# Pre-norm weights as columns on the transposed x, and x / rms made by ScalarE, in a two-layer decoder trunk

## The chip, the core and the metric

The kernel runs on one core of a Trainium2 chip. The metric is the device time of one execution, in microseconds: lower is better. The engines work side by side, each through its own queue in order: TensorE (PE, with its weight loads as PEld) multiplies matrices into PSUM, VectorE (DVE) and ScalarE (ACT) work elementwise, GpSimd (POOL) makes the inverse roots, and SyncE (SP) only issues DMAs.

## The reference

One sequence of 512 tokens with 1024 channels in float32 goes through two layers of three residual stages. The first and third are SwiGLU feed-forward blocks with 2816 hidden channels, the second a mixer of attention, a short convolution and a pooling branch. Each stage is wrapped in two RMS norms, one ahead of it and one behind it, each with weights g per channel:

```python
def _rmsnorm(x, g):
    x32 = x.astype(jnp.float32)
    y = x32 * lax.rsqrt(jnp.mean(x32 * x32, axis=-1, keepdims=True) + RMS_EPS)
    return (y * g.astype(jnp.float32)).astype(x.dtype)
...
    for l in range(DEPTH):
        g = norm_g[l]
        f = _swiglu(_rmsnorm(x, g[0]), ffn_w_gate[l, 0], ffn_w_up[l, 0], ffn_w_down[l, 0])
        x = x + 0.5 * _rmsnorm(f, g[1])
        m = _mixer(_rmsnorm(x, g[2]), w_in[l], conv_w[l], pool_w[l], pool_scale[l], w_out[l])
        x = x + _rmsnorm(m, g[3])
        f = _swiglu(_rmsnorm(x, g[4]), ffn_w_gate[l, 1], ffn_w_up[l, 1], ffn_w_down[l, 1])
        x = x + 0.5 * _rmsnorm(f, g[5])
```

## The kernel before

The residual x stays in SBUF as four token tiles of 128 tokens by 1024 channels. A stage needs the normed x with channels on the partitions, so each token tile is transposed by TensorE. Every float32 matrix is split into a high part (rounded to TensorE's float32r format) and the rest, and a product is three matmuls: high by high, high by rest, rest by high (`mm3`). For the normed x the parts are `hHs` (named hh in the trace) and `hLs` (hl); for weights wh and wl.

**Weights and slots.** All weights come in 324 units of up to 128 x 1024. `load` (L145 to L149) issues a unit's DMA on SP into a slot named raw, `split` makes wh with ScalarE (L156) and wl with VectorE (L157). There are 28 slots of 512 KB for raw, wh, wl, the parts of hidden activations, accumulators f, and the norm weights. A ledger in Python counts them while the program is written: `ahead` loads a unit while more slots are free than `slots["reserve"]`, and splits one while at least two more are free than that; it runs whenever slots are given back (`give`). This fixes the order in which loads and splits stand in the program. The order of the instructions in each queue is then settled when the program is built; for TensorE it is chained by hand (`after`), in the order of the listing.

**A stage's end.** There are six ends; the change touches the five that have a stage behind them. In the feed-forward block the last chunk, in the mixer the second half of the output projection (`OUT_B`), runs token tile by token tile (`by_tokens`), each tile in two halves of 512 channels. `Boundary` loads the post-norm weights (`self.post`) and the weights of the norm ahead of the next stage (`self.g`), each a 128 x 1024 tile with the same row in all partitions (`gain`, L207 to L211, 512 KB, one slot). For each half tile `store` adds the last product to f (L363), sums squares with ScalarE (L364) and multiplies by the post weights (L367). `finish` makes the mean (L373), the inverse root on POOL (`root`, L314) and adds to x (L377), and calls `prenorm`: two squares with sums by ScalarE (L322), x times the weights (L323), the mean (L324), the root, and the scaling (L326), all into f's slot. `turned` runs as a side task 13 us of matmuls later (`D_TURN`): eight transposes (L267) in two groups of four into PSUM banks, a ScalarE copy to hh (L335) and a VectorE subtraction to hl (L336) for each group. Then it gives back f's slot, and with the last tile those of the two weight tiles.

**The stage behind** a mixer end is a feed-forward block. Its first three pairs of units run on token tiles 0 and 1 alone before they run on 2 and 3 (`HEAD`), so hh and hl of tiles 0 and 1 must exist when it starts. Behind a feed-forward stage of the same layer the mixer takes one token tile at a time.

**The first norm** (`first`, at the start) already works in another way: x / rms is transposed without weights, and a column of weights per channel group, from the tile `cst`, is multiplied on the way out of PSUM (L818), before the copy (L820) and the subtraction (L821).

Of the kernel before, what the change touches and what calls it, by code (L numbers as in the profile page):

```python
# [15 lines left out]
P = 128  # L16
# [8 lines left out]
DEPTH = 2  # L25
# [33 lines left out]
C_G0 = C_PSC + DEPTH * 2  # L59
C_END = C_G0 + KB  # L60

# [41 lines left out]
def trunk_kernel(ctx: ExitStack, tc: tile.TileContext, xt: bass.AP, wu: bass.AP,  # L103
# [81 lines left out]

    cst = cpool.tile([P, 64], F32, name="cst")[:, :C_END]
    x = cpool.tile([P, TBS, D], F32, name="x")
# [128 lines left out]

    def prenorm(key, tb, g, buf, free):

        ss, ms = small(), small()
        for dh in range(2):  # L320
            s = slice(dh * DH, (dh + 1) * DH)
            nc.scalar.activation(tmp(), x[:, tb, s], AF.Square, scale=D ** -0.5, accum_out=ss[:, dh:dh + 1])  # L322
        nc.vector.tensor_tensor(buf, x[:, tb, :], g, op=ALU.mult)  # L323
        nc.vector.scalar_tensor_tensor(ms[:, 0:1], ss[:, 0:1], EPS, ss[:, 1:2], op0=ALU.add, op1=ALU.add)  # L324
        r = root(ms[:, 0:1])
        nc.vector.tensor_scalar(buf, buf, r, None, op0=ALU.mult)  # L326

        def turned():
            for q in range(2):
                ps = bank()  # L330
                for i in range(4):
                    turn(ps[:, i * P:(i + 1) * P], buf[:, (4 * q + i) * P:(4 * q + i + 1) * P])
                pv = ps.rearrange("p (a b) -> p a b", a=4)
                dst = (slice(None), slice(4 * q, 4 * q + 4), tok(tb))
                nc.scalar.copy(hHs[dst], pv)  # L335
                nc.vector.tensor_tensor(hLs[dst], pv, f32(hHs[dst]), op=ALU.subtract)  # L336
            done((key, "h", tb))
            free()
            return
            yield  # L340

        side(turned(), D_TURN)

    class Boundary:


        def __init__(self, n, l, i, pre):
            self.key, self.pre = n + 1, pre
            self.post = gain(l, i + 1)
            self.g = gain(*pre) if pre is not None else None  # L350

            factor = 1.0 if i == 2 else 0.5
            self.scale, self.eps = D ** -0.5 / factor, EPS / factor ** 2
            self.left = TBS
            self.ss, self.fg = {}, {}
# [15 lines left out]
        def finish(self, tb, f):  # L371
# [8 lines left out]
            if self.pre is not None:  # L380
                prenorm(self.key, tb, self.g, f, self.free)

        def free(self):
            self.left -= 1
            slots["reserve"] += 1
            give(1 if self.left else 3)

# [53 lines left out]
    def ffn(n_, l, i, pre, next_reserve):  # L441
# [13 lines left out]
        for c, n in enumerate(CHUNKS):  # L455
            last = c == len(CHUNKS) - 1
            if last:
                slots["reserve"] += 2 if pre is not None else 1
                bd = Boundary(n_, l, i, pre)
# [135 lines left out]
    def mixer(key, l, i, pre):  # L595
# [179 lines left out]
        need((key, "mix"))  # L775
        slots["reserve"] += 2
        give(TBS)
# [26 lines left out]
    def first(tb, buf):  # L804
# [6 lines left out]

        for q in range(2):
            ps = bank()
            for i in range(4):
                turn(ps[:, i * P:(i + 1) * P], buf[:, (4 * q + i) * P:(4 * q + i + 1) * P])
            g = cst[:, C_G0 + 4 * q:C_G0 + 4 * q + 4].unsqueeze(2).to_broadcast((P, 4, P))
            t = tmp().rearrange("p (a b) -> p a b", a=4)
            nc.vector.tensor_tensor(t, ps.rearrange("p (a b) -> p a b", a=4), g, op=ALU.mult)  # L818
            dst = (slice(None), slice(4 * q, 4 * q + 4), tok(tb))
            nc.scalar.copy(hHs[dst], t)  # L820
            nc.vector.tensor_tensor(hLs[dst], t, f32(hHs[dst]), op=ALU.subtract)  # L821
        if tb == 0:
# [71 lines left out]
def _pack_consts(norm_g, conv_w, pool_scale):  # L894
# [8 lines left out]
    c[:, C_PSC:C_PSC + DEPTH * 2] = pool_scale.reshape(DEPTH * 2, P).T  # L903
    c[:, C_G0:C_G0 + KB] = norm_g[0, 0].reshape(KB, P).T
    return c
# [37 lines left out]
```

## Time and profile before

| | us |
|---|---|
| median of 3 runs | 1924.6 |
| lowest and highest | 1923.42, 1925.09 |
| the profiled execution, its time | 1924.39 |
| its span, first to last instruction | 1922.6 |
| VectorE, ScalarE and POOL busy | 875.8, 719.6, 44.6 |

The page of the profile gives the busy time of each engine, its share in 40 equal slices of the span and the granted clock of TensorE (1.00 is 2.4 GHz, 0.50 is 1.2 GHz). A timeline lists instructions in order of time; a bracket behind one gives the idle time of its engine just before it and what ended that. Matmuls overlap, so a row's duration is longer than the distance to the next start. Names are those of the program without buffer numbers; L12 is line 12.

### The profile page before, as it was taken

The page shows a single profiled execution, that of the slowest core. Times are in us where ns is not written, and L with a number is a line of the kernel's source. Part 1 is how long each engine was busy: PE and PEld are TensorE (multiplying, and loading weights), DVE is VectorE, ACT ScalarE, POOL GpSimd, SP SyncE. Part 2 cuts the span into 40 slices and gives each one's busy share as a digit, 9 for nine tenths or more (in the row PEclk, how much of TensorE's full clock was granted, in tenths as well). Part 3 has the DMA queues.
Part 4 walks back from the last instruction along what each step waited for, and adds up shares of the span by engine and source line. Part 5 has one row for each costly group of instructions (what it writes and reads, how often), then busy time and mean ns, then how long its engine had stood idle before and what let it go on. Part 6 is the DMA issues. An engine that isn't in the chain of part 4 may idle for free.

```text
span 1922.6 us, 22108 instructions
## 1 busy us (share of the span) xinstructions
PE 1887.2 (98%) x9078; PEld 1590.5 (83%) x9078; DVE 875.8 (46%) x1158; ACT 719.6 (37%) x1129; POOL 44.6 (2%) x68
## 2 busy tenths in 40 slices
PE   7999999999999999999999999999999999999998
PEld 6888888888878888888898888888888888888887
DVE  5323333567767323333463223337577663223333
ACT  4323222357764323222243322224477542322221
POOL 0000000000001000000000000000000010000000
PEclk8999999999999999999999999999999999999999
DMA  5223232131123223223142322423211232222311
GB/s 196 99 73 125 77 117 103 44 132 55 38 88 127 93 72 121 84 102 121 44 153 78 109 88 77 142 77 107 70 50 44 83 142 89 99 88 88 132 66 44
DMA packets 50501, 179.65 MB, mean 93 GB/s; under 512 B 5728, under 2 KB 5856, under 8 KB 50400
## 3 DMA queue, kind: packets, MB, share of 16 engines
q1 hardware_dynamic: 50400, 178.24, 26.8%
q8 instruction: 71, 1.16, 0.2%
q14 instruction: 30, 0.25, 0.0%
HBM read 176.12 MB, written 2.10 MB: 93 GB/s over the span
## 4 chain that ended last, share of the span: by engine, by line
PE 90%; DVE 6%; ACT 1%; issue 1%; DMA 1%; POOL 0%; SPq 0%; DVEq 0%; POOLq 0%; ACTq 0%
PE psz L225 78%; PE psd L225 11%; DVE wl L157 1%; DMA g<-in_gains_dram 1%; PE psd L267 1%; DVE f L363 1%; DVE x L377 1%; DVE f L323 1%; ACT t L298 0%; DMA raw<-in_w_dram 0%; DVE pL L514 0%; DVE hl L336 0%; ACT pH L513 0%; POOL ss L314 0%; ACT t L543 0%
## 5 line engine op out<-in xcount | busy, mean ns | idle before, releaser
L225 PE MATMUL psz<-hh,wh 128*128 128x512 f32 (+1 forms) x1536 | 569.0, 370 | 7.0 <-ACT hh L335 4.2
L225 PE MATMUL psz<-hl,wh 128*128 128x512 f32 (+1 forms) x1536 | 568.4, 370 | 5.4 <-DVE hl L336 4.3
L225 PE MATMUL psz<-hh,wl 128*128 128x512 f32 (+1 forms) x1536 | 567.8, 370 | 0.0
L157 DVE TENSOR_TENSOR wl<-raw,wh 128x1024 fp32r<-128x1024 f32 x324 | 386.9, 1210 | 313.9 <-ACT wh L156 245.8
L225 PE MATMUL psz<-wh,hid 128*128 128x512 f32 x1408 | 437.4, 390 | 0.0
L156 ACT CAST wh<-raw 128x1024 fp32r<-128x1024 f32 x324 | 328.8, 1039 | 224.0 <-PE psz L225 177.9
L225 PEld LDWEIGHTS psz<-hh,wh 128*128 128x128 f32 x1536 | 293.6, 191 | 55.6 <-ACT hh L335 5.1
L225 PEld LDWEIGHTS psz<-hl,wh 128*128 128x128 f32 x1536 | 293.6, 191 | 53.3 <-DVE hl L336 5.0
L225 PEld LDWEIGHTS psz<-hh,wl 128*128 128x128 f32 x1536 | 293.4, 191 | 47.1
L225 PEld LDWEIGHTS psz<-wh,hid 128*128 128x128 f32 x1408 | 264.5, 188 | 54.6
L449 DVE TENSOR_TENSOR t<-t,psz 128x512 f32<-128x512 f32 x84 | 57.7, 687 | 479.4 <-PE psz L225 479.4
L225 PE MATMUL psz<-wl,hid 128*128 128x512 f32 x704 | 274.3, 390 | 0.0
L450 ACT CAST hid<-t 128x512 fp32r<-128x512 f32 x88 | 54.6, 620 | 450.8 <-DVE t L449 450.8
L298 ACT ACTIVATE t<-psz 128x512 f32<-128x512 f32 (+1 forms) x136 | 77.4, 573 | 236.0 <-PE psz L225 235.1
L225 PEld LDWEIGHTS psz<-wl,hid 128*128 128x128 f32 x704 | 132.3, 188 | 27.0
L225 PE MATMUL psd<-hh,wh 128*128 128x512 f32 (+1 forms) x320 | 119.8, 374 | 0.0
L225 PE MATMUL psd<-hh,wl 128*128 128x512 f32 (+1 forms) x320 | 118.2, 369 | 0.0
L225 PE MATMUL psd<-hl,wh 128*128 128x512 f32 (+1 forms) x320 | 118.1, 369 | 0.0
L451 DVE TENSOR_TENSOR hid<-t,hid 128x512 fp32r<-128x512 f32 x88 | 61.0, 693 | 60.8 <-ACT hid L450 60.8
L314 POOL TENSOR_TENSOR ss<-ss,expo 128x1 f32<-128x1 f32 x48 | 36.1, 752 | 1691.9 <-DVE ss L373 1582.6
L225 PEld LDWEIGHTS psd<-hl,wh 128*128 128x128 f32 x320 | 60.5, 189 | 10.1 <-issue 0.5
L225 PEld LDWEIGHTS psd<-hh,wl 128*128 128x128 f32 x320 | 60.4, 189 | 10.2
(106 smaller groups left out, 1435.4 us busy)
## 6 DMA issues: line engine op xcount, KB each, us to landing
raw<-in_w_dram SPq DMA_DIRECT2D x316, 512.0 KB, 3.3
g<-in_gains_dram SPq DMA_DIRECT2D x11, 512.0 KB, 5.1
x<-in_xt_dram SPq DMA_DIRECT2D x4, 512.0 KB, 6.9
raw<-in_w_dram SPq DMA_DIRECT2D x8, 256.0 KB, 2.8
out_dram<-x SPq DMA_DIRECT2D x8, 256.0 KB, 2.1
mat<-in_mats_dram SPq DMA_DIRECT2D x1, 384.0 KB, 9.1
mat<-in_mats_dram SPq DMA_DIRECT2D x1, 64.0 KB, 3.2
cst<-in_consts_dram SPq DMA_DIRECT2D x1, 29.0 KB, 3.2
```

Of the source, the lines that this page charges most:

```text
L156: nc.scalar.copy(h[:, :n], raw[:, :n])
L157: nc.vector.tensor_tensor(lo[:, :n], raw[:, :n], f32(h[:, :n]), op=ALU.subtract)
L225: ins = nc.tensor.matmul(dst, w, r, start=start, stop=stop, skip_group_check=True)
L267: ins = nc.tensor.transpose(dst, src, ident)
L298: ins = nc.scalar.activation(out_, in_, f_, **kw)
L314: nc.gpsimd.tensor_tensor(r, ms, expo, op=ALU.pow)
L323: nc.vector.tensor_tensor(buf, x[:, tb, :], g, op=ALU.mult)
L363: nc.vector.tensor_tensor(f[:, s], f[:, s], ps, op=ALU.add)
L377: nc.vector.scalar_tensor_tensor(xs, self.fg.pop((tb, dh)), r, xs, op0=ALU.mult, op1=ALU.add)
L449: nc.vector.tensor_tensor(u, g, pu, op=ALU.mult)
L450: nc.scalar.copy(t[:, 0, :], u)
L451: nc.vector.tensor_tensor(t[:, 1, :], u, f32(t[:, 0, :]), op=ALU.subtract)
```

## The change

The weights of all six norms ahead of a stage now lie as columns in `cst`, which grows from 58 to 98 columns. `prenorm` no longer multiplies by the weights and makes x / rms with one ScalarE activation (identity with the root as a scale per token) instead of VectorE's L326. The way out of PSUM that `first` had becomes `turned_parts`, used by `turned` as well: VectorE multiplies each group of four transposes by its columns into a temporary tile, ScalarE copies that to hh, VectorE subtracts to hl. `Boundary` loads no pre-norm weights; the ledger reserves one slot at a stage's end instead of two, and the last token tile gives back two instead of three.

```diff
--- before.py
+++ after.py
@@ -57,7 +57,7 @@
 C_CONV = C_INV16 + 2 * PAD
 C_PSC = C_CONV + DEPTH * 2 * 3
 C_G0 = C_PSC + DEPTH * 2
-C_END = C_G0 + KB
+C_END = C_G0 + DEPTH * 3 * KB
 
 M_ID, M_TRI, M_MASK, M_POOL = 0, P, 2 * P, 3 * P
 M_END = M_POOL + DEPTH * 2 * P
@@ -183,7 +183,7 @@
 
 
 
-    cst = cpool.tile([P, 64], F32, name="cst")[:, :C_END]
+    cst = cpool.tile([P, 128], F32, name="cst")[:, :C_END]
     x = cpool.tile([P, TBS, D], F32, name="x")
     mat = cpool.tile([P, M_END], F32, name="mat")
     hHs = cpool.tile([P, KB, T], F32R, name="hh")
@@ -314,26 +314,32 @@
         nc.gpsimd.tensor_tensor(r, ms, expo, op=ALU.pow)
         return r
 
-    def prenorm(key, tb, g, buf, free):
+    def turned_parts(n, tb, buf):
+
+        for q in range(2):
+            ps = bank()
+            for i in range(4):
+                turn(ps[:, i * P:(i + 1) * P], buf[:, (4 * q + i) * P:(4 * q + i + 1) * P])
+            o = C_G0 + n * KB + 4 * q
+            g = cst[:, o:o + 4].unsqueeze(2).to_broadcast((P, 4, P))
+            t = tmp().rearrange("p (a b) -> p a b", a=4)
+            nc.vector.tensor_tensor(t, ps.rearrange("p (a b) -> p a b", a=4), g, op=ALU.mult)
+            dst = (slice(None), slice(4 * q, 4 * q + 4), tok(tb))
+            nc.scalar.copy(hHs[dst], t)
+            nc.vector.tensor_tensor(hLs[dst], t, f32(hHs[dst]), op=ALU.subtract)
+
+    def prenorm(key, tb, buf, free):
 
         ss, ms = small(), small()
         for dh in range(2):
             s = slice(dh * DH, (dh + 1) * DH)
             nc.scalar.activation(tmp(), x[:, tb, s], AF.Square, scale=D ** -0.5, accum_out=ss[:, dh:dh + 1])
-        nc.vector.tensor_tensor(buf, x[:, tb, :], g, op=ALU.mult)
         nc.vector.scalar_tensor_tensor(ms[:, 0:1], ss[:, 0:1], EPS, ss[:, 1:2], op0=ALU.add, op1=ALU.add)
         r = root(ms[:, 0:1])
-        nc.vector.tensor_scalar(buf, buf, r, None, op0=ALU.mult)
+        nc.scalar.activation(buf, x[:, tb, :], AF.Identity, scale=r)
 
         def turned():
-            for q in range(2):
-                ps = bank()
-                for i in range(4):
-                    turn(ps[:, i * P:(i + 1) * P], buf[:, (4 * q + i) * P:(4 * q + i + 1) * P])
-                pv = ps.rearrange("p (a b) -> p a b", a=4)
-                dst = (slice(None), slice(4 * q, 4 * q + 4), tok(tb))
-                nc.scalar.copy(hHs[dst], pv)
-                nc.vector.tensor_tensor(hLs[dst], pv, f32(hHs[dst]), op=ALU.subtract)
+            turned_parts(key, tb, buf)
             done((key, "h", tb))
             free()
             return
@@ -347,7 +353,6 @@
         def __init__(self, n, l, i, pre):
             self.key, self.pre = n + 1, pre
             self.post = gain(l, i + 1)
-            self.g = gain(*pre) if pre is not None else None
 
             factor = 1.0 if i == 2 else 0.5
             self.scale, self.eps = D ** -0.5 / factor, EPS / factor ** 2
@@ -378,12 +383,12 @@
                 if self.pre is None:
                     nc.sync.dma_start(out=out[:, tb, dh * DH:(dh + 1) * DH], in_=xs)
             if self.pre is not None:
-                prenorm(self.key, tb, self.g, f, self.free)
+                prenorm(self.key, tb, f, self.free)
 
         def free(self):
             self.left -= 1
             slots["reserve"] += 1
-            give(1 if self.left else 3)
+            give(1 if self.left else 2)
 
 
     def token_mms(ps, tb, src, blocks, w, dh_first, dh_last):
@@ -455,7 +460,7 @@
         for c, n in enumerate(CHUNKS):
             last = c == len(CHUNKS) - 1
             if last:
-                slots["reserve"] += 2 if pre is not None else 1
+                slots["reserve"] += 1
                 bd = Boundary(n_, l, i, pre)
             src = {}
             j = 0
@@ -773,7 +778,7 @@
         by_halves(OUT_A, mixed, store)
         give(3)
         need((key, "mix"))
-        slots["reserve"] += 2
+        slots["reserve"] += 1
         give(TBS)
         load_set(18)
         bd = Boundary(key, l, i, pre)
@@ -809,16 +814,7 @@
         r = root(ms[:, 0:1])
         nc.vector.tensor_scalar(buf, x[:, tb, :], r, None, op0=ALU.mult)
 
-        for q in range(2):
-            ps = bank()
-            for i in range(4):
-                turn(ps[:, i * P:(i + 1) * P], buf[:, (4 * q + i) * P:(4 * q + i + 1) * P])
-            g = cst[:, C_G0 + 4 * q:C_G0 + 4 * q + 4].unsqueeze(2).to_broadcast((P, 4, P))
-            t = tmp().rearrange("p (a b) -> p a b", a=4)
-            nc.vector.tensor_tensor(t, ps.rearrange("p (a b) -> p a b", a=4), g, op=ALU.mult)
-            dst = (slice(None), slice(4 * q, 4 * q + 4), tok(tb))
-            nc.scalar.copy(hHs[dst], t)
-            nc.vector.tensor_tensor(hLs[dst], t, f32(hHs[dst]), op=ALU.subtract)
+        turned_parts(0, tb, buf)
         if tb == 0:
             ps = bank("z")
             for _ in range(WARM // 4):
@@ -901,7 +897,7 @@
             c[rows, C_INV16 + b * PAD:C_INV16 + (b + 1) * PAD] = 1.0 / np.minimum(np.arange(1, PAD + 1), w)
     c[:, C_CONV:C_CONV + DEPTH * 6] = conv_w.reshape(DEPTH, 3, 2, P).transpose(3, 0, 2, 1).reshape(P, DEPTH * 6)
     c[:, C_PSC:C_PSC + DEPTH * 2] = pool_scale.reshape(DEPTH * 2, P).T
-    c[:, C_G0:C_G0 + KB] = norm_g[0, 0].reshape(KB, P).T
+    c[:, C_G0:C_END] = norm_g[:, 0::2].reshape(DEPTH * 3 * KB, P).T
     return c
```

## Rows read from the trace of the kernel before

**Rows 1.** The page, part 1: busy us, share of the span, instructions, by engine.

```profile
PE 1887.2 (98%) x9078; PEld 1590.5 (83%) x9078; DVE 875.8 (46%) x1158; ACT 719.6 (37%) x1129; POOL 44.6 (2%) x68
```

**Rows 2.** Table by stretch: us, busy us (instructions) of five engines, granted clock, DMA.

```profile
30.00:378.00 348.00, 348.00 (x1653) 294.03 (x1653) 120.83 (x135) 97.24 (x130) 2.08 (x3) 0.99 0.26 90
...
560.00:624.00 64.00, 59.84 (x330) 52.51 (x330) 44.65 (x63) 32.27 (x62) 7.13 (x8) 0.95 0.41 144
...
1505.00:1570.00 65.00, 60.62 (x336) 53.04 (x337) 45.68 (x65) 32.45 (x63) 7.14 (x8) 0.97 0.40 142
```

**Rows 3.** TensorE's timeline at both mixer ends: start us, us, instruction, idle before and releaser.

```profile
599.26 1.03 PE L267 MATMUL psd<-mat,f 128*128 128x128 f32 x8
...
600.59 0.40 PE L225 MATMUL psz<-wh,mix 128*128 128x512 f32 x1
...
603.30 0.41 PE L225 MATMUL psz<-hh,wh 128*128 128x256 f32 x1 [2.31 <-ACT hh L335]
...
605.57 0.58 PE L225 MATMUL psz<-hl,wh 128*128 128x256 f32 x1 [1.85 <-DVE hl L336]
...
1548.97 0.38 PE L225 MATMUL psz<-hh,wh 128*128 128x256 f32 x1 [1.89 <-ACT hh L335]
...
1551.47 0.39 PE L225 MATMUL psz<-hl,wh 128*128 128x256 f32 x1 [2.12 <-DVE hl L336]
```

**Rows 4.** TensorE alone, six us behind each stall and at full clock: busy, clock.

```profile
605.57:611.57 6.00, 6.00 (x32) 0.60 0.38 150
1551.47:1557.47 6.00, 6.00 (x37) 0.72 0.32 127
613.60:619.60 6.00, 6.00 (x53) 1.00 0.33 122
```

**Rows 5.** TensorE's timeline at the three other stage ends.

```profile
396.62 0.63 PE L267 MATMUL psd<-mat,f 128*128 128x128 f32 x4 [0.51 <-DVE f L326]
...
972.76 0.38 PE L225 MATMUL psz<-hl,wh 128*128 128x256 f32 x1 [0.33 <-DVE hl L336]
...
1342.69 0.52 PE L267 MATMUL psd<-mat,f 128*128 128x128 f32 x3 [0.50 <-DVE f L326]
```

**Rows 6.** Groups by line: engine, operation, out<-in, shapes, count, busy us, mean ns, idle before.

```profile
L156 ACT CAST wh<-raw 128x1024 fp32r<-128x1024 f32 x324 | 328.8, 1039 | 224.0 <-PE psz L225 177.9 <-DVE wl L157 23.5 <-DMA raw<-in_w_dram 19.9
...
L336 DVE TENSOR_TENSOR hl<-psd,hh 128x512 fp32r<-128x512 f32 x40 | 25.8, 684 | 12.3 <-ACT hh L335 12.3
...
L323 DVE TENSOR_TENSOR f<-x,g 128x1024 f32<-128x1024 f32 x20 | 24.4, 1221 | 0.3
...
L498 ACT COPY f<-psz 128x512 f32<-128x512 f32 x32 | 18.7, 586 | 62.0 <-PE psz L225 62.0
...
L326 DVE TENSOR_SCALAR f<-f,ss 128x1024 f32<-128x1024 f32 x20 | 15.0, 751 | 6.0 <-POOL ss L314 6.0
...
L818 DVE TENSOR_TENSOR t<-psd,cst 128x512 f32<-128x512 f32 x8 | 5.2, 684 | 0.0
...
L710 ACT ACTIVATE mix<-psd,cst 128x512 fp32r<-128x512 f32 x4 | 2.7, 686 | 0.6 <-PE psd L225 0.6
```

**Rows 7.** VectorE's timeline at the end of layer 0's mixer.

```profile
579.44 0.69 DVE L367 TENSOR_TENSOR t<-f,g 128x512 f32<-128x512 f32 x1 [3.11 <-DMA g<-in_gains_dram]
...
593.43 0.68 DVE L363 TENSOR_TENSOR f<-f,psz 128x512 f32<-128x512 f32 x1
...
594.03 0.75 DVE L326 TENSOR_SCALAR f<-f,ss 128x1024 f32<-128x1024 f32 x1
...
604.82 1.28 DVE L336 TENSOR_TENSOR hl<-psd,hh 128x512 fp32r<-128x512 f32 x2
```

**Rows 8.** SP's queue at that end; then both gain loads: KB, us to landing.

```profile
572.37 0.90 SPq L210 DMA_DIRECT2D g<-in_gains_dram  x2
...
g<-in_gains_dram SPq DMA_DIRECT2D x1, 512.0 KB, 7.0
...
g<-in_gains_dram SPq DMA_DIRECT2D x1, 512.0 KB, 7.7
```

## The prediction

> **What bounds the kernel now.** I read the busy shares first. TensorE is busy 1887.2 us of a span of 1922.6 [rows 1], so no change off TensorE can give back more than the 35.4 us in which it stands still, plus what it loses by running at a lower clock. The page's slices give an average; the table of stages says where those 35 us lie. In the body of a feed-forward stage there is nothing to win: 348.00 of 348 us are TensorE's. The stretches around the end of each token mixer are different: 59.84 of 64 us, and 60.62 of 65, with a granted clock of 0.95 and 0.97 [rows 2]. So I went to TensorE's own instructions there, looking for the bracket that tells how long it stood and who released it. In layer 0 the last matmul of the mixer's output projection starts at 600.59 and ends at 600.99. The first matmul of the next feed-forward stage starts at 603.30 (2.31 us idle, released by the ScalarE copy of L335 that makes hh), and the next at 605.57 (1.85 us, released by VectorE's L336 that makes hl). Layer 1 has the same pair, 1.89 and 2.12 us [rows 3]. Both instructions are the last steps of `turned`, on token tile 1, which this change rewrites.
>
> The idle time has a second price. Behind the stall the granted clock is at 1.2 GHz for some microseconds: in the six microseconds after the restart TensorE gets 32 and 37 matmuls done, against 53 of the same matmuls in six microseconds at 2.4 GHz [rows 4]. That is 6 x (1 - 32/53) = 2.4 us and 6 x (1 - 37/53) = 1.8 us. The prize at the two mixer ends is therefore 4.16 + 4.01 = 8.2 us idle and 4.2 us of slow clock, 12.4 us in all. The other three ends hold little: 0.51 and 0.50 us where the transposes of token tile 2 wait for x / rms (L326), and 0.33 us at the end between two feed-forward stages [rows 5]. The order of TensorE's instructions is written out by hand and the change adds and removes none of them, so it moves only these waits.
>
> **Who makes the stall.** VectorE's instructions in layer 0 show it. It waits 3.11 us for the post-norm weights, starts on them at 579.44, and has hardly a gap from there until hl of token tile 1 at 604.82 [rows 7]. That subtraction could have begun at about 600.6: the first four transposes, which start at 599.26 [rows 3], are through at about 599.9, and one copy of 0.59 us [rows 6] stands between. It begins 4.2 us late because VectorE is behind. What counts is VectorE's work ahead of 604.82.
>
> **The change, part by part.** Durations are of the profiled execution, 1924.4 us with a span of 1922.6; the median of the three runs is 1924.6, so a forecast against the one serves for the other.
>
> *VectorE.* Each of the 20 token tiles of five stage ends loses the weight multiply L323 (1.22 us) and the scaling L326 (0.75 us), and gains two multiplies out of PSUM like L818 (0.68 us each) [rows 6]: 0.6 us less. L336 becomes a subtraction of the same size from SBUF; I cost that at nothing. At a mixer end more goes than that before the critical hl: three L323 (token tiles 0 to 2) and two L326, 5.16 us, against four added multiplies, 2.74 us: 2.4 us less, if the order of the queue stays.
>
> *ScalarE.* x / rms becomes one 128x1024 activation scaled by a column. The trace has no such form. Below it stands the cast of the same size, 1.04 us; a scale by a column costs L710 0.10 us more than the plain copy L498 (686 against 586 ns), which makes 1.14; two of L710 would be 1.37 [rows 6]. I take 1.14, the nearest row plus the measured surplus, so x / rms is 0.39 us longer than L326. It waits for POOL's root, and casts, squares and hh copies queue behind it on ScalarE, which is 32 of 64 us busy there [rows 2]. The cover is the distance to the transposes: in layer 0 x / rms of token tile 1 is done at 594.78 [rows 7] and its transposes run at 599.26 [rows 3], 4.5 us later. Without that cover it would cost 0.39 us a token. The Trainium skill ("ScalarE: Activation LUTs", Rules for kernel authors) speaks against this move: multiplies belong on VectorE. The trace agrees for the instruction alone, 1.04 us for ScalarE's cast of that size against L326's 0.75 [rows 6].
>
> *The chain behind the transposes* gets longer by one instruction and one hand-over: multiply, copy, subtract, 0.68 + 0.59 + 0.68 = 1.95 us where it was 1.27. With every engine prompt hl of token tile 1 is then ready at about 599.9 + 2.1 = 602.0 (the hand-overs taken as 0.15 us), so a mixer end keeps some 1.0 us idle even in the best case, 3.1 us less than now.
>
> *DMAs and slots.* Five loads of 512 KB (the pre-norm weights) go. They stand behind the post-norm weights on SP's queue; landings come in the order of issue (post weights 7.0 us after 572.37, pre weights 7.7 us after about 572.9, 1.2 us later [rows 8]), so their removal brings the post weights no earlier. The reserve of one slot instead of two does the opposite. Counted along the listing, 5 slots are free after `give(TBS)` in `mixer` (L777). With a reserve of 2, `ahead` takes one split and one load (5, 4, 3) and then lacks a slot for the second split; with a reserve of 1 it takes two splits and two loads (5, 4, 3, 2, 1). One more 512 KB load thus stands ahead of the post weights, which take the place that the pre weights had: they land 1.2 us later, at about 580.6, and VectorE's backlog starts 1.2 us later. It is bounded by nothing (the load finds its slot too late and goes behind) and about 3 us (the weights wait for a slot that a split gives back); I take 1.2. In a feed-forward stage the post weights are loaded long before their use; there the slot only lets weights run one load further ahead, and TensorE never waited for those [rows 2].
>
> *cst* grows from 29 to 49 KB and is loaded behind the first tile of x; it is used after a root, a scaling and transposes. Cost nothing, bound 0.1 us.
>
> **The sum.** At a mixer end no more than 3.1 us can be gained (the chain). The other bound is VectorE's queue in its present order. VectorE catches up with TensorE by token tile 2's last addition, which runs at 593.43 now [rows 7] and is due when TensorE has finished that tile, about 592.2: back from 600.99 by token tile 3's two halves of 15 matmuls (twice as wide as those of [rows 4], so 0.23 us each) and two groups of eight transposes (1.0 us a group [rows 3]). That is 1.2 us earlier. From there to the critical hl one L326 and one L323 go and four multiplies come, 2.74 - 0.75 - 1.22 = 0.8 us more, so 0.4 us is gained. I cannot see the new order of the queues and take the middle, 1.75 us an end, 3.5 in all. Of the slow clock's 4.2 us I take back a third, 1.4: it fell behind some 4 us of idle, and rather over 2 would be left. The two waits for x / rms (1.0 us) should go, since the sum of squares no longer waits behind L323, but the longer chain may put 0.4 us back there and 0.4 at the end between feed-forward stages: 0.2 gained. 1924.4 - 3.5 - 1.4 - 0.2 = **1919.3 us**, within 1916 to 1921.
>
> **The rivals.**
>
> *Full relief*: the queues run so that hl is made as soon as its inputs exist, both stalls shrink to 1.0 us and the clock stays up: 6.2 + 4.2 us gained, 1914.0. For it: 2.4 us less work on an engine that is 4.2 late. Against it: one more hand-over on a full engine, and the weights 1.2 us later.
>
> *Swallowed*: the added multiplies and the weight splits stand ahead of hl in VectorE's queue, 0.4 us an end is gained and the clock falls as before: 1924.4 - 0.8 = 1923.6.
>
> *Slower*: VectorE doesn't catch up. It works in order, and each token's finish holds it in a wait for POOL's root, so the 1.2 us by which the weights come late reach hl at both ends, and the extra multiply and hand-over add 0.8 us: 4.0 us. The end between feed-forward stages, where TensorE already waits for hl [rows 5], pays the same 0.8: 1924.4 + 4.8 = 1929.2. It decides from the point at which the last addition of token tile 2 stands more than about 1 us after TensorE's end of that tile.
>
> *ScalarE late*: the scaling by a column waits in ScalarE's queue and the transposes wait for it, 0.39 us at each of five ends, 2.0 us off the gain: 1921.3. The cover of 4.5 us speaks against its being paid. The Trainium skill's rule ("ScalarE: Activation LUTs", Rules for kernel authors) would have it so. The trace bears out its price [rows 6], not its place.
>
> **How the numbers follow.** Forecast 0.45, full relief 0.13, swallowed 0.26, slower 0.12, ScalarE late 0.04. The likeliest gives 1919.3. The range takes in full relief, swallowed and slower: 1914 to 1929; a full relief with more at the other ends, and a slower case with the clock down for longer, are left out. A measurement of this kernel tells 0.2% (3.9 us) from no change, so faster means under 1920.6: 0.38 of the forecast's 0.45, and 0.13 of full relief: 0.51. Same: 0.07 of the forecast, 0.24 of swallowed, 0.04 of ScalarE late, 0.02 of slower: 0.37. Slower: 0.10 and 0.02 of swallowed: 0.12.
>
> **What would show it.** Right: at the two mixer ends TensorE's idle brackets sum to 1 to 3 us; the first weighted product waits for post weights that land near 580.6, with one more weight load between the last one of now and them; the rows of tile 2's transposes lose their bracket; the new ScalarE line takes 1.1 us. Wrong: brackets of 4 us as now (swallowed), idle brackets in front of transposes, released by ScalarE (ScalarE late), or new brackets before hh at the feed-forward ends. The forecast rests most on the order in the queues of VectorE and ScalarE, which the trace of before cannot show.

## The result, and the profile after

The changed kernel is slower. Its median is 1948.05 us (1947.66 to 1949.28) against 1924.84 us of the kernel before, a ratio of 1.0129 with a 95% interval of 1.0117 to 1.0141. The forecast was 1919.3 us, 1914 to 1929.

The page's busy line, to be held against [rows 1]:

```profile
PE 1891.0 (97%) x9078; PEld 1592.6 (82%) x9078; DVE 865.8 (44%) x1158; ACT 743.5 (38%) x1149; POOL 46.4 (2%) x68
```

VectorE has 10.0 us less to do and ScalarE 23.9 more, as planned. TensorE has the same 9078 matmuls and is busy 3.8 us longer; the span is 24.0 us longer. The rest is TensorE standing still. Its timeline at the ends of layer 0's mixer, the end between two feed-forward stages, the end at 1360 us and layer 1's mixer end (the bracket is the idle time and its releaser), against [rows 3, 5]:

```profile
601.39 0.40 PE L225 MATMUL psz<-wh,mix 128*128 128x512 f32 x1
609.70 0.58 PE L225 MATMUL psz<-hh,wh 128*128 128x256 f32 x1 [7.91 <-ACT hh L328]
612.12 0.58 PE L225 MATMUL psz<-hl,wh 128*128 128x256 f32 x1 [1.83 <-DVE hl L329]
...
985.93 0.58 PE L225 MATMUL psz<-hh,wh 128*128 128x256 f32 x1 [7.01 <-ACT hh L328]
987.27 0.58 PE L225 MATMUL psz<-hl,wh 128*128 128x256 f32 x1 [0.76 <-DVE hl L329]
...
1360.23 0.99 PE L267 MATMUL psd<-mat,f 128*128 128x128 f32 x7 [1.26 <-ACT f L339]
...
1572.38 0.58 PE L225 MATMUL psz<-hh,wh 128*128 128x256 f32 x1 [7.76 <-ACT hh L328]
1574.79 0.58 PE L225 MATMUL psz<-hl,wh 128*128 128x256 f32 x1 [1.83 <-DVE hl L329]
```

The mixer ends go from 4.16 and 4.01 us of idle to 9.74 and 9.59, the feed-forward end from 0.33 to 7.77, the wait at 1360 us from 0.50 to 1.26: 19.4 us together, and with the 3.8 us of slower matmuls nearly all of the 24.0. The slower matmuls follow the stalls. TensorE alone, six us behind the last of each (busy, count, granted clock, then DMA share and GB/s), against [rows 4]:

```profile
612.12:618.12 6.00, 6.00 (x32) 0.59 0.25 85
987.27:993.27 6.00, 6.00 (x31) 0.57 0.06 23
1574.79:1580.79 6.00, 6.00 (x32) 0.60 0.22 80
```

The middle row is new. In the kernel before TensorE did 50 matmuls at a clock of 1.00 in the six us behind its 0.33 us there:

```profile
972.76:978.76 6.00, 6.00 (x50) 1.00 0.94 367
```

The releaser of the long stalls is ScalarE's copy to hh of token tile 1, so the first reading goes to ScalarE's timeline at layer 0's mixer end, with POOL's root under it:

```profile
606.10 1.15 ACT L339 ACTIVATE f<-x,ss 128x1024 f32<-128x1024 f32 x1 [2.31 <-POOL ss L314]
607.15 1.97 ACT L156 CAST wh<-raw 128x1024 fp32r<-128x1024 f32 x2
609.03 1.13 ACT L328 CAST hh<-t 128x512 fp32r<-128x512 f32 x2
```
```profile
596.59 0.55 POOL L314 TENSOR_TENSOR ss<-ss,expo 128x1 f32<-128x1 f32 x1 [2.07 <-DVE ss L378]
602.86 3.20 POOL L314 TENSOR_TENSOR ss<-ss,expo 128x1 f32<-128x1 f32 x1 [5.72 <-DVE ss L337]
```

ScalarE waits 2.31 us for the root of token tile 2, which takes 3.20 us where the one before it took 0.55, then scales tile 2 (L339), then casts two units of weights, and only then copies hh of tile 1. VectorE's timeline in the same stretch tells another story:

```profile
582.43 1.29 DVE L372 TENSOR_TENSOR t<-f,g 128x512 f32<-128x512 f32 x2 [2.44 <-DMA g<-in_gains_dram]
...
604.98 0.68 DVE L372 TENSOR_TENSOR t<-f,g 128x512 f32<-128x512 f32 x1
605.58 1.27 DVE L326 TENSOR_TENSOR t<-psd,cst 128x512 f32<-128x512 f32 x2
606.78 0.67 DVE L368 TENSOR_TENSOR f<-f,psz 128x512 f32<-128x512 f32 x1
607.37 3.48 DVE L157 TENSOR_TENSOR wl<-raw,wh 128x1024 fp32r<-128x1024 f32 x3
610.78 0.68 DVE L372 TENSOR_TENSOR t<-f,g 128x512 f32<-128x512 f32 x1
611.38 1.28 DVE L329 TENSOR_TENSOR hl<-t,hh 128x512 fp32r<-128x512 f32 x2
```

Three things are to be seen. The post-norm weights come 3.0 us later than in [rows 7] (582.43 against 579.44). The multiplies of tile 1 run at 605.58, although its transposes were over by about 601.1. And between them and hl stand three weight splits in a row, 3.4 us. Counted from the first weighted product to hl of tile 1, VectorE does six splits here; in the kernel before it does four. At the end between the feed-forward stages it does seven, before three. The rows give VectorE's splits (L157) alone in these two stretches (us, busy, count, clock, DMA), of the changed kernel and then of the kernel before:

```profile
582.43:611.38 28.95, 7.12 (x6) 0.92 0.36 128
949.30:986.53 37.23, 8.45 (x7) 0.94 0.35 117
```
```profile
579.44:604.82 25.38, 4.89 (x4) 0.97 0.35 120
942.70:972.02 29.32, 3.65 (x3) 1.00 0.19 59
```

### The profile page after: what moved, and what is told of

The parts are those of the page before. It is cut to its first block, busy times and chain, and to the rows that moved or that the text cites. A ratio compares the mean times of both kernels' runs of the same rounds, so it can differ in the third digit from the quotient of the medians.

```text
span 1946.6 us, 22117 instructions
## 1 busy us (share of the span) xinstructions
PE 1891.0 (97%) x9078; PEld 1592.6 (82%) x9078; DVE 865.8 (44%) x1158; ACT 743.5 (38%) x1149; POOL 46.4 (2%) x68
## 4 chain that ended last, share of the span: by engine, by line
PE 89%; DVE 5%; DMA 2%; ACT 2%; issue 1%; POOL 0%; SPq 0%; DVEq 0%; POOLq 0%; ACTq 0%
PE psz L225 78%; PE psd L225 10%; DMA raw<-in_w_dram 2%; DVE wl L157 2%; PE psd L267 1%; ACT t L298 0%; DVE t L326 0%; DVE pL L519 0%; DVE t L551 0%; DVE hl L329 0%; ACT pH L518 0%; ACT t L548 0%; ACT wh L156 0%; POOL ss L314 0%; ACT f L339 0%
## 5 line engine op out<-in xcount | busy, mean ns | idle before, releaser
L157 DVE TENSOR_TENSOR wl<-raw,wh 128x1024 fp32r<-128x1024 f32 x324 | 386.7, 1209 | 299.3 <-ACT wh L156 251.6
```

What stands on the lines that cost most here:

```text
L157: nc.vector.tensor_tensor(lo[:, :n], raw[:, :n], f32(h[:, :n]), op=ALU.subtract)
```

## The theories

A: ScalarE. x / rms waits for POOL's root in ScalarE's queue, and hh of the tile before it waits behind. B: the multiply as an added step, in two forms, D and E. D, place: hh and hl become ready one step later, and when the program is built the queues fill that time with weight splits, behind which hh and hl then stand. E, length: the longer chain costs this wherever it stands. C: the one-slot ledger, which lands the post-norm weights later.

Idle time below is that of TensorE at the three ends in the order mixer of layer 0, between the feed-forward stages, mixer of layer 1, in brackets over 0.3 us; the kernel before has 4.16, 0.33 and 4.01. In e4, e5, e7, e9, e11 and e13 to e15 the middle one stands in front of transposes; in the others, in front of the first products.

| kernel | median us | ratio to before (95%) | idle us |
|---|---|---|---|
| after | 1948.05 | 1.0129 (1.0117 to 1.0141) | 9.74, 7.77, 9.59 |
| e1_scale_dve | 1949.10 | 1.0132 (1.0117 to 1.0147) | 10.42, 7.79, 10.40 |
| e2_two_slots | 1941.59 | 1.0090 (1.0073 to 1.0107) | 8.09, 8.09, 8.11 |
| e3_mult_only | 1945.21 | 1.0112 (1.0097 to 1.0127) | 8.81, 7.40, 9.72 |
| e4_scale_act | 1924.95 | 1.0011 (1.0002 to 1.0021) | 2.79, 0.94, 3.84 |
| e5_one_slot | 1934.44 | 1.0050 (1.0031 to 1.0069) | 2.34, 2.29, 2.67 |
| e6_mult_order | 1924.48 | 1.0002 (0.9992 to 1.0011) | 4.35, 0, 4.35 |
| e7_after_order | 1932.37 | 1.0044 (1.0029 to 1.0059) | 6.62, 1.06, 6.69 |
| e8_before_order | 1922.50 | 0.9992 (0.9979 to 1.0004) | 2.86, 0, 3.12 |
| e9_two_order | 1924.46 | 1.0003 (0.9994 to 1.0012) | 3.22, 1.07, 3.25 |
| e10_before_late | 1932.25 | 1.0048 (1.0035 to 1.0060) | 6.28, 1.74, 6.53 |
| e11_before_back3 | 1916.28 | 0.9962 (0.9949 to 0.9974) | 1.26, 0.85, 1.27 |
| e12_mult_back3 | 1920.35 | 0.9985 (0.9975 to 0.9995) | 2.72, 0, 3.80 |
| e13_two_back3 | 1921.66 | 0.9990 (0.9981 to 1.0000) | 2.42, 0.79, 2.42 |
| e14_early_post | 1926.76 | 1.0014 (1.0006 to 1.0023) | 4.73, 1.06, 4.36 |
| e15_early_post3 | 1923.27 | 1.0001 (0.9992 to 1.0010) | 3.26, 0.78, 3.56 |

## Experiments: the parts of the change one by one

**e1_scale_dve**, x / rms back on VectorE:

```diff
-        nc.scalar.activation(buf, x[:, tb, :], AF.Identity, scale=r)
+        nc.vector.tensor_scalar(buf, x[:, tb, :], r, None, op0=ALU.mult)
```

> The changed kernel, but x / rms is made by VectorE again (x times the root, into f's slot); columns on the way out of PSUM and the one-slot ledger stay. Theory A: at the mixer ends x / rms of token tile 2 stands ahead of the hh copies of tile 1 in ScalarE's queue and holds it 2.3 us for POOL's root and 1.15 us for itself. Then hh of tile 1 follows its multiply and two casts, 2 to 3 us earlier: the stall before it falls from 7.8 us to about 5.3 at each mixer end, from 7.0 to about 5.5 at the end between feed-forward stages, the wait for x / rms at 1360 us goes, and the time is about 1948 - 2.5 x 2 - 1.5 - 0.8 - 1 (clock) = 1940 us. Theory B (the multiply as an added step ahead of hh is the cause, wherever x / rms is made): within 2 us of 1948. Theory C (the post-norm weights, 3.0 us later, are the cause): within 2 us of 1948, the stalls as they are.

Nothing is gained: 1949.10 us. TensorE's timeline at layer 0's mixer end:

```profile
606.00 0.58 PE L225 MATMUL psz<-hh,wh 128*128 128x256 f32 x1 [5.18 <-ACT hh L328]
611.82 0.58 PE L225 MATMUL psz<-hl,wh 128*128 128x256 f32 x1 [5.24 <-DVE hl L329]
```

The stall before hh shrinks by 2.7 us, just as A said, and the stall before hl grows by 3.4: hl starts at 611.08 us on VectorE, still behind three splits. ScalarE's wait was real and bound nothing. A falls as the cause.

**e2_two_slots**, the ledger of before on the changed kernel:

```diff
     self.post = gain(l, i + 1)
+    if pre is not None:
+        slots["reserve"] -= 1
+        slots["free"] -= 1
...
-    slots["reserve"] += 1
+    slots["reserve"] += 2
```

> The changed kernel with the slot ledger of before: two slots are reserved at a stage's end, the second one counted and not used. Theory C: the post-norm weights land at about 579.4 again and not at 582.3, VectorE's work at the mixer ends starts 3.0 us earlier, and up to that much goes from each of the two stalls of 9.7 us: 1948 - 2 x 3 = 1942 us, lower if the clock stays up; the end between feed-forward stages keeps its 7.8 us. Theory A: what counts is ScalarE's queue; VectorE's and POOL's chain before the root of tile 2 starts with the weights, so some of it comes back, 1 to 3 us an end, but the idle time of ScalarE in front of x / rms of tile 2 stays. Theory B: 0 to 2 us an end.

6.5 us less than the changed kernel: 3.1 us of idle at the mixer ends, the two waits for x / rms behind the feed-forward stages (0.58 and 1.26 us), which are gone, and smaller ones. C is a part, over a quarter of the loss, and not all of it by the way that it named.

**e3_mult_only**, both edits together:

> The changed kernel with both undone, x / rms by VectorE and the ledger of before: of the change only the columns on the way out of PSUM are left (and the pre-norm weights are neither loaded nor multiplied ahead of the transposes). Theory A and C together: about the kernel before, 1924.8 plus the longer chain behind the transposes at three ends (0.8 us each at most), 1922 to 1928. Theory B: the stalls of the mixer ends stay over 6 us each and that between the feed-forward stages over 4 us, 1936 us or more.

1945.21 us. With x / rms on VectorE, the ledger of before and nothing else of the change but the columns out of PSUM (with them L323 and the loads of the pre-norm weights are gone), 21 us of the loss are there. VectorE's timeline has the three splits again:

```profile
600.54 1.28 DVE L326 TENSOR_TENSOR t<-psd,cst 128x512 f32<-128x512 f32 x2
601.74 0.68 DVE L371 TENSOR_TENSOR f<-f,psz 128x512 f32<-128x512 f32 x1
602.34 0.74 DVE L339 TENSOR_SCALAR f<-x,ss 128x1024 f32<-128x1024 f32 x1
603.00 3.49 DVE L157 TENSOR_TENSOR wl<-raw,wh 128x1024 fp32r<-128x1024 f32 x3
606.41 0.68 DVE L375 TENSOR_TENSOR t<-f,g 128x512 f32<-128x512 f32 x1
607.01 1.28 DVE L329 TENSOR_TENSOR hl<-t,hh 128x512 fp32r<-128x512 f32 x2
```

**e4_scale_act**, the kernel before with only its scaling on ScalarE:

```diff
-        nc.vector.tensor_scalar(buf, buf, r, None, op0=ALU.mult)
+        nc.scalar.activation(buf, buf, AF.Identity, scale=r)
```

> The kernel before with one part of the change: the scaling by the root (x times weights, in place) goes from VectorE to ScalarE. No multiply behind the transposes, weights and ledger as before. Theory A in its plain form (ScalarE waiting for the root holds the hh copies): slower by 3 us or more at each mixer end, 1931 us or above. Theory B: hh of tile 1 has no multiply ahead of it and keeps its place in front of tile 2's scaling, so nothing is lost there: 1923 to 1926, with the waits for x / rms at the two ends behind the feed-forward stages of 0.5 us grown to 1 to 1.5 us.

1924.95 us, 0.1% above the kernel before (interval 0.02 to 0.21%): at most a small part of the loss. It is B, then, and the next four ask whether by place or by length.

## Experiments: place or length

The order is fixed with the kernel's own `after`, which orders two instructions and adds no wait on data. For token tile 1 at every end the two splits listed before its turn, and those listed from there until tile 2's turn, are put behind its last hh (ScalarE) and its last hl (VectorE). Nothing is added or removed:

```diff
+    def behind(c, v):
+        after(c, hold["hh"], "split behind hh")
+        after(v, hold["hl"], "split behind hl")
...
+        if hold["on"]:
+            behind(c, v)
+        hold["splits"].append((c, v))
...
             turned_parts(key, tb, buf)
+            hold["on"] = tb == 1
+            if tb == 1:
+                for c, v in hold["splits"][-2:]:
+                    behind(c, v)
```

**e6_mult_order** is e3_mult_only with it.

> The kernel of e3_mult_only, with the order in two queues fixed for token tile 1 at each end: hh and hl stand ahead of the weight splits (L156, L157) that now stand between its multiplies and its hl; the last two splits listed before it and those listed until the next tile's turn are put behind it. Nothing else changes. Theory D (place): the multiply itself costs little; what costs is that hh and hl, ready one step later, are queued behind three more splits at a mixer end (3 x 1.14 us of VectorE) and behind six at the end between feed-forward stages. Then the stalls fall from 8.8 us to about 5 at the mixer ends and from 7.4 to under 2 at the other, and the time from 1945 to about 1945 - 2 x 3.7 - 6 - 2 (clock) = 1930 us. Theory E (length): the longer chain and the two extra instructions cost this wherever they stand: 1942 us or more, stalls within 1.5 us of those of e3_mult_only.

1924.48 us, 20.7 less than e3_mult_only and level with the kernel before. VectorE's timeline at the same place (line numbers are 8 to 12 higher):

```profile
600.50 1.29 DVE L334 TENSOR_TENSOR t<-psd,cst 128x512 f32<-128x512 f32 x2
601.69 0.68 DVE L383 TENSOR_TENSOR f<-f,psz 128x512 f32<-128x512 f32 x1
602.29 0.76 DVE L347 TENSOR_SCALAR f<-x,ss 128x1024 f32<-128x1024 f32 x1
602.95 0.69 DVE L337 TENSOR_TENSOR hl<-t,hh 128x512 fp32r<-128x512 f32 x1
```

The multiplies stand where they stood in e3_mult_only, and hl starts 4.1 us earlier, at 602.95 and not 607.01. The end between the feed-forward stages, 7.40 us of idle there, has none. Every instruction of the longer chain is still there: E falls, D holds.

**e7_after_order** is the whole changed kernel with it.

> The changed kernel with the same order fixed for token tile 1. Theory D: the three splits (3.4 us of VectorE) go from in front of hl at each mixer end and six from in front of it between the feed-forward stages; ScalarE's wait for the root of tile 2 stays ahead of hh there: stalls of about 6 us at the mixer ends and 1 to 3 between the feed-forward stages, 1948 - 2 x 3.5 - 5.5 - 2 = about 1933 us. If x / rms on ScalarE is the larger part once the splits are out of the way, it is 4 us or more above e6_mult_order plus the 3 us that the ledger costs at each mixer end. Theory E: within 3 us of 1948.

1932.37 us, 15.7 less than the changed kernel, the 1933 that D gave. The edit moves hh on ScalarE and hl on VectorE together, so these two runs do not tell what each is worth.

**e8_before_order** is the kernel before with it.

> The kernel before with the same order fixed for token tile 1. In its own order one split fewer or so stands ahead of hl of tile 1 than without the edges. Theory D: hl comes 1 to 2 us earlier at the mixer ends, 1924.5 - 2 to 4 = 1920 to 1922 us, and the 0.3 us between the feed-forward stages goes. Theory E has nothing to say on it; if the edges alone cost or gain something else (a split too late for TensorE), it shows here as a new stall on wh or wl.

1922.50 us; its interval includes a ratio of 1, so no gain is shown. Its stalls fall by about 1 us each (to 2.86 and 3.12).

**e10_before_late** turns it round: the kernel before with hl of tile 1 behind the last split listed ahead of it and the next one.

```diff
+            if tb == 1:
+                for c, v in hold["splits"][-1:]:
+                    for x_ in hls:
+                        after(x_, v, "hl behind split")
+                hold["late"] = hls
```

> The kernel before, with the place of hl alone made worse: hl of token tile 1 is put behind the last split listed before it and the next one listed, two more than stand ahead of it now at the mixer ends and one more at the end between feed-forward stages. No multiply, no ScalarE scaling, ledger as before. Theory D: 2 x 1.14 us at each mixer end and 1.2 to 1.5 at the other, with as much slow clock as before: 1924 + 4.6 + 1.3 = about 1930 us. If place counts for little in the kernel before: 1923 to 1926.

1932.25 us, 8.6 more than before. Six splits now stand ahead of hl at the mixer ends, as many as in the changed kernel, and four at the end between the feed-forward stages. The place of hl alone, with no part of the change, makes a third of its loss. VectorE's and TensorE's timelines there:

```profile
605.50 2.36 DVE L158 TENSOR_TENSOR wl<-raw,wh 128x1024 fp32r<-128x1024 f32 x2
607.78 1.28 DVE L342 TENSOR_TENSOR hl<-psd,hh 128x512 fp32r<-128x512 f32 x2
```
```profile
604.09 0.58 PE L230 MATMUL psz<-hh,wh 128*128 128x256 f32 x1 [2.43 <-ACT hh L341]
608.52 0.58 PE L230 MATMUL psz<-hl,wh 128*128 128x256 f32 x1 [3.85 <-DVE hl L342]
```

## Experiments: the ledger, and what the change is worth in a good order

**e5_one_slot**, the kernel before with the one-slot ledger:

```diff
-            self.g = gain(*pre) if pre is not None else None
+            self.g = self.post
...
-        slots["reserve"] += 2
+        slots["reserve"] += 1
```

> The kernel before with the ledger of the changed one: one slot reserved, and no load of the pre-norm weights; the multiply ahead of the transposes stays and reads the post-norm weights in their place, so the result has the wrong weights and the work is the same. Theory C (the ledger alone delays the post-norm weights by 3 us): these land at about 582.3 us in layer 0, and the stall of each mixer end grows from 4.1 us to about 7: 1924.5 + 2 x 3 = 1930.5 us. If the 3 us came from the queues of the changed kernel and not from the ledger: 1923 to 1926.

1934.44 us (1928.98 to 1936.07; the profile is of the fastest of its four executions), and it settles nothing. The post-norm weights land at 583.99 us, but the mixer ends have less idle than before, not more, and TensorE waits 2.3 to 2.5 us at three places that no theory named, in front of transposes behind the feed-forward stages. Its queues came out in another order, so it is no test of one thing.

**e9_two_order** is e7_after_order with the ledger of before.

> The changed kernel with the order fixed for token tile 1 (as in e7_after_order) and with the slot ledger of before (as in e2_two_slots): the columns and x / rms on ScalarE are left. e7_after_order stands 8 us above e6_mult_order; this splits them. If the ledger makes it (3 us later post-norm weights at two ends, 6.5 us between the changed kernel and e2_two_slots): 1925 to 1927 us, stalls of 3 us at the mixer ends. If ScalarE's wait for the root of tile 2 ahead of hh makes it: 1930 to 1932, with hh released by ScalarE 2 us or more behind the multiply.

1924.46 us: the ledger makes the whole of the 7.9 us. Against e6_mult_order, where VectorE scales, x / rms on ScalarE neither costs nor gains (1924.46 and 1924.48).

**e14_early_post** is e7_after_order with one line moved up in `mixer`:

```diff
         slots["reserve"] += 1
+        bd = Boundary(key, l, i, pre)
         give(TBS)
         load_set(18)
-        bd = Boundary(key, l, i, pre)
```

> As e7_after_order (the changed kernel with the order fixed for token tile 1, one-slot ledger), but in the mixer the post-norm weights are loaded ahead of the weights that the returned slots let run ahead. If the ledger costs by the late landing: the post-norm weights of layer 0 land at about 577 us or earlier and not at 581.6, the stalls of 6.0 us shrink to about 3, and the time is that of e9_two_order, 1923 to 1926 us. If it costs by the one more split that stands ahead on VectorE: within 2 us of e7_after_order's 1932.

1926.76 us: 5.6 of the 7.9 us come back. The weights land at 575.98 us in place of 581.56. The 2.3 us left are the other way that the theory named. VectorE has three splits between the last x update of tile 1 (L394) and hl of tile 0, where e9_two_order has two, and the idle before hh is longer by one split at both ends (4.39 against 3.22 in layer 0):

```profile
592.97 1.42 DVE L394 SCALAR_TENSOR_TENSOR x<-t,ss,x 128x512 f32<-128x512 f32 x2 [0.66 <-POOL ss L322]
594.30 1.22 DVE L162 TENSOR_TENSOR wl<-raw,wh 128x1024 fp32r<-128x1024 f32 x1
...
597.23 1.22 DVE L162 TENSOR_TENSOR wl<-raw,wh 128x1024 fp32r<-128x1024 f32 x1
598.37 0.15 DVE L345 SCALAR_TENSOR_TENSOR ss<-ss 128x1 f32<-128x1 f32 x1
598.44 1.22 DVE L162 TENSOR_TENSOR wl<-raw,wh 128x1024 fp32r<-128x1024 f32 x1
599.58 1.29 DVE L337 TENSOR_TENSOR hl<-t,hh 128x512 fp32r<-128x512 f32 x2
```

Four more put three splits, not two, behind tile 1 (`[-3:]`).

**e11_before_back3**, the kernel before:

> As e8_before_order (the kernel before with the order fixed), with one more split put behind hl of token tile 1. Theory D: 1.1 us less stall at each mixer end than in e8_before_order (2.9 us there), and less slow clock behind it: about 1922.5 - 2.2 - 1.5 = 1919 us, faster than the kernel before. If the stalls go and the time doesn't, the lost weights show as new stalls on wh or wl behind it.

**e12_mult_back3**, the columns alone:

> As e6_mult_order (columns only, x / rms on VectorE, ledger of before), with one more split put behind hh and hl of token tile 1: at a mixer end none of those listed since tile 0's turn is left between tile 1's transposes and its hl but the first. Theory D: 1.1 us less stall at each mixer end than in e6_mult_order (4.4 us there), 1924.5 - 2.2 - 1 = about 1921 us, a shade faster than the kernel before. If what is left there is the chain (transposes, multiply, copy, subtract): as e6_mult_order.

**e13_two_back3**, columns and ScalarE:

> As e9_two_order (columns, x / rms on ScalarE, ledger of before, order fixed), with one more split put behind hh and hl of token tile 1. Theory D: the one stall left at each mixer end, 3.2 us before hh, gets 1.1 us shorter: 1924.5 - 2.2 - 1 = about 1921 us. If the change's 2.4 us less on VectorE ahead of hl is worth anything once the order is the same, it is at or under the 1916 us of e11_before_back3; if the added multiply and hand-over and the wait for the root eat it, it is 3 us or more above.

**e15_early_post3**, the whole change with the post-norm weights first:

> As e14_early_post, with the one more split put behind hh and hl of tile 1: the whole change, its ledger too, with the order fixed and the post-norm weights loaded first. As e13_two_back3 if the landing is all that the ledger costs, about 1921 us; 1929 or so if it is not.

e11_before_back3 takes 1916.28 us (0.9962, 0.9949 to 0.9974): it beats both kernels, and it has no part of the change. The three others take 1920.35, 1921.66 and 1923.27. So in this order the columns alone take 4 us more than a kernel without them, and the whole change 7. Whether another order would suit the change better, no run shows. TensorE's timeline in e11_before_back3 and the six us behind it, then the same of e13_two_back3:

```profile
600.87 0.38 PE L233 MATMUL psz<-hl,wh 128*128 128x256 f32 x1 [1.26 <-DVE hl L344]
...
600.87:606.87 6.00, 6.00 (x50) 1.00 0.83 329
```
```profile
604.17 0.38 PE L233 MATMUL psz<-hh,wh 128*128 128x256 f32 x1 [2.08 <-ACT hh L336]
604.90 0.39 PE L233 MATMUL psz<-hl,wh 128*128 128x256 f32 x1 [0.34 <-DVE hl L337]
...
604.90:610.90 6.00, 6.00 (x37) 0.72 0.55 214
```

2.42 us of idle are left where the kernel without the change leaves 1.26. The added step (multiply, copy, subtract) is not all of the difference. In e13_two_back3 the copies to hh also stand behind x / rms of tile 2 on ScalarE, which waits for POOL's root:

```profile
602.46 1.15 ACT L347 ACTIVATE f<-x,ss 128x1024 f32<-128x1024 f32 x1 [1.50 <-POOL ss L322]
603.52 1.12 ACT L336 CAST hh<-t 128x512 fp32r<-128x512 f32 x2
```

In e12_mult_back3, where VectorE makes x / rms, 2.72 and 3.80 us are left; what the added step costs by itself stays open. Behind 2.42 us the clock is down for part of the next six, behind 1.26 us it is not, by the two rows above. TensorE's busy time over the whole span says the same: 1886.6 us in e13_two_back3, 1881.7 in e11_before_back3, 1887.2 in the kernel before.

## Why the prediction was wrong

**Where the prize lies: right.** e11_before_back3 takes most of it: 2.5 us of idle left at the mixer ends of 8.2, TensorE 5.5 us less busy, 7.4 us of time out of the 12.4 forecast as the prize.

**VectorE's saving: right in size, wrong in use.** The multiply took 682 ns, the subtraction 685 (0.68 forecast). But "2.4 us less, if the order of the queue stays" put everything on its condition, and it did not stay: in front of hl of tile 1 in layer 0, six splits stand where four stood, and at the feed-forward end seven where three did. This is the step that failed. The forecast counted the instructions that the change adds and removes and let the others keep their places. A step added between the transposes and hh makes hh and hl ready later, and the splits that are ready then go ahead. All four kernels with the multiply and no fixed order (after, e1, e2, e3) have six and seven; before and e4, without it, have four and three, and e5 has four and four. That the queue is filled because hl is not ready yet is my reading of this: the four also lack L323 and the loads of the pre-norm weights, and no run separates these from the multiply. That the place costs what it costs is shown, by e6_mult_order and e7_after_order one way and e10_before_late the other.

**A part of the saving became waiting.** Between the first weighted product and hl of tile 1, VectorE's brackets over 0.3 us add up to 1.8 us before and 4.7 after, all for POOL's roots and ScalarE's sums of squares. L323 had stood in the wait for the squares of x, which now shows (0.79 us). And twice VectorE waits 0.91 us for the squares of f (L369), which stand behind x / rms (L339) on ScalarE; in e3_mult_only, where VectorE scales, that wait is 0.12 us. The sum took L323's and L326's whole time as gained.

**Post-norm weights: mis-sized.** 1.2 us was taken and the bound of 3 us came true, for the reason written beside it: the load went out at 578.98 us, as soon as a split gave back a slot, and not at 572.37. With the one more split on VectorE the ledger cost 6.5 to 7.9 us (e2, e9); the sum had no own term for it.

**ScalarE.** x / rms took 1148 ns (1.14 forecast). Its cover was measured to its own transposes only; that the hh copies queue behind it stood in the text and had no price. The trace shows that queueing, and by e1 and by e9 against e6 it cost nothing here; without the fixed order it even gained 3.6 us (e2 against e3). The rule of the Trainium skill ("ScalarE: Activation LUTs", Rules for kernel authors) that puts multiplies on VectorE agrees in the price of one instruction, 1148 ns against L326's 751 [rows 6], and not in the time of the kernel.

**The end between the feed-forward stages: missed.** 0.4 us was allowed; it lost 7.4 and a slow clock behind it that it never had. It was priced by the chain, and the same mechanism hit it harder. The prediction had named new brackets before hh at these ends as a sign of being wrong.

**The chain.** Its best case, 1.0 us idle at a mixer end, was never reached: 2.42 us are left in e13_two_back3, with hh and hl ahead of three splits and x / rms of tile 2 still ahead of hh.

**The rivals.** "Slower" named late weights and the added step and priced them at 4.8 us; its mechanism for the second, an extra 0.8 us, was the chain and not the splits. Its 1929 us was 19 short. "Swallowed" did name the weight splits ahead of hl, but let them cost only the gain: it held 1923.6 us.

**The account.** Order 15.7 us (after to e7_after_order), ledger 7.9 (to e9_two_order), together 23.6 of 23.2 us; what is left of the change is then level with the kernel before, within the runs' spread. These are prices in this sequence of edits: with the order left free the ledger was worth 6.5 us (e2), and the kernel before gains by a fixed order as well, so that in the same order columns and ScalarE together still stand 2 us (e9 against e8) to 5.4 us (e13 against e11) behind.

## What to carry to other kernels

An instruction added to a chain costs its duration only if the queues keep their order: look up which ready work of the same engines stands next to the chain in the trace (here weight splits of 1.1 us each), and price the forecast with that work ahead of the chain as well. Where the first waiting instruction has a clear releaser, look at what the next one waits for before believing it; taking away ScalarE's wait only moved the stall from hh to hl. And where an order matters, write it into the kernel: the kernel before gained 7.4 us by that, more than the 5.1 us that the forecast expected of the change.

## What the runs showed that was not expected

POOL's root of one number per partition takes 0.55 us or up to 3.20, and the rows beside it show when. In the changed kernel the one at 602.86 ends at 606.06, 0.48 us after VectorE's multiply out of PSUM starts at 605.58; from 602.64 to 605.58 VectorE had run nothing but instructions with two inputs in SBUF (wl, hl, the weighted product). The same holds in e3_mult_only (597.83 to 601.03, the multiply at 600.54) and e6_mult_order (598.92 to 600.99, at 600.50); in the kernel before the root at 605.05 takes 0.55 beside an hl that reads PSUM, and the one at 610.46, beside two splits, 2.53. No run tests it by itself. The Trainium skill ("SBUF — State Buffer", SBUF: two separate sides) has the rule: a VectorE instruction with two SBUF inputs and a GpSimd instruction that reads SBUF contend for one pair of ports, and whoever has it holds it for the whole instruction. These rows agree, and in them a run of such instructions on VectorE kept the root waiting for all its length. By this reading, moving hl's input from PSUM to SBUF, which the prediction costed at nothing, can lengthen a root that runs beside it; the splits and the weighted product in the same run do so too.
